# Seven block products in place of eight: the gate and up products of a SwiGLU layer on one Trainium2 core

## The chip, the cores and the metric

The kernel runs on one core of one Trainium2 chip. The metric is the time of one execution on the device, in microseconds. TensorE appears as PE in the rows (its weight loads as PEld), VectorE as DVE, ScalarE as ACT, GpSimd as POOL, and SyncE, which issues nearly all transfers, as SP.

## The reference

One layer over 512 latent tokens of width 2048, with 256 context tokens, all in float32:

```python
h = modulate(rms_norm(x, norm_mix), mod[:, 0], mod[:, 1])
p = h @ w_in                        # then three mixers, merged and projected by w_out
x = x + mod[:, 2] * latent_mixer(p, rope, k_ctx, v_ctx, lw)
h2 = modulate(rms_norm(x, norm_ffn), mod[:, 3], mod[:, 4])
x = x + mod[:, 5] * swiglu(h2, lw)

def swiglu(h, lw):
    return (jax.nn.silu(h @ lw["w_ffn_gate"]) * (h @ lw["w_ffn_up"])) @ lw["w_ffn_down"]
```

The change concerns the last two lines of the layer. `w_ffn_gate` and `w_ffn_up` are 2048 x 5632, `w_ffn_down` is 5632 x 2048.

## The kernel before, in words

Channels lie on the 128 partitions and tokens along the free axis, so the moving operand of a product is 128 channels x 512 tokens and the stationary operand a 128 x 128 block of a weight. Every float32 operand is split into two fp32r parts: ScalarE casts it to `hi`, VectorE subtracts to get `lo` (`split_load`, lines 69 and 70, for weights; `split_to`, lines 82 and 83, for other tiles). A product is then three matmuls into the same PSUM bank, `hi*hi`, `lo*hi` and `hi*lo` (`mm3`, lines 77 to 79).

`proj_pair` (line 523) makes 256 output channels: it loads four 128-row blocks of a weight (512 KB) with one transfer, splits them, and runs 24 matmuls on them. Its staging tiles `raw`, `whi` and `wlo` have three buffers each. Weights come on SP's queue.

After the output projection `w_out` (tile `pwo`, line 829) the kernel sums squares over all channels (`pms`), takes the reciprocal root on GpSimd, spreads it over the partitions with four small matmuls into `ptb` (line 856), and makes the normalised and modulated tokens `h2h`/`h2l` tile by tile: one multiply on VectorE, one biased copy on ScalarE, one fused subtract on VectorE (lines 865 to 867).

The feed-forward part then runs in 11 chunks of 512 hidden channels. `gate_up(c)` makes the gate (`pfg`) and up (`pfu`) products, applies silu, multiplies and splits the result. `down(c - 1)` multiplies the chunk before with `w_ffn_down` and adds it, scaled, to the residual `xn`, which stays in SBUF. In the last chunk each finished pair of channels is transposed back (`pto`) and stored.

The scheduler of the framework orders the instructions of each engine from its own estimate. Only in stretches marked `manual_schedule` does an engine keep the order of the source; the feed-forward part has none before.

Of the kernel before, what the change touches and what calls it, by code (L numbers as in the profile page):

```python
# [18 lines left out]
P = 128  # L19
T = 512  # L20
D = 2048
KT = D // P
# [11 lines left out]
def hybrid_block(ctx: ExitStack, tc: tile.TileContext, I, out):  # L34
# [83 lines left out]
    spg = [dram.tile([P, 512], F32, name=f"spg{i}") for i in range(KT)]  # L118

# [693 lines left out]
    ex.close()  # L813
    ex = ExitStack()
    ep = ex.enter_context(tc.tile_pool(name="ep2", bufs=2, side="right", reuse_waits="tile"))
    xn = [None] * 8
# [3 lines left out]
    pms = bank("tp", "pms", 2)  # L820

# [4 lines left out]
    for j in range(8):  # L826
        xr = ep.tile([P, 2, 512], F32, tag="xr", name="xr", bufs=2)
        nc.sync.dma_start(xr, spx[j])
        po = proj_pair(I["w_out"][0], 256 * j, KT, mk, "pwo")
        xn[j] = yt(f"xn{j}", F32)  # L830
        xa[j] = ep.tile([P, 2, 512], F32, tag="xa", name=f"xa{j}", bufs=8)
        if j == 7:
            sumsq(sqa, True, False)
        for n in range(2):
            kt = 2 * j + n
            nc.vector.scalar_tensor_tensor(xn[j][:, n], po[n], modc[:, 0, kt:kt + 1], xr[:, n], op0=mul, op1=add)
            if kt == 0:
                nc.scalar.activation(sqa, xn[j][:, n], AF.Square)
            else:
                s = t2("sq2")  # L840
                nc.scalar.activation(s, xn[j][:, n], AF.Square)
                if j < 7:
                    nc.gpsimd.tensor_tensor(sqa, sqa, s, op=add)
                else:
                    sumsq(s, False, n == 1)
        for n in range(2):
            nc.scalar.activation(xa[j][:, n], xn[j][:, n], AF.Copy, scale=a2[:, 2 * j + n:2 * j + n + 1])
# [10 lines left out]
    h2h, h2l = [], []  # L858
    for c in range(8):
        h2h.append(act(f"h2h{c}", F32R))  # L860
        h2l.append(act(f"h2l{c}", F32R))
        for j in range(2):
            kt = 2 * c + j
            u = t2("u2")
            nc.vector.tensor_tensor(u, xa[c][:, j], rb2, op=mul)
            nc.scalar.activation(h2h[c][:, j], u, AF.Identity, bias=modc[:, 1, kt:kt + 1])  # L866
            nc.vector.scalar_tensor_tensor(h2l[c][:, j], u, modc[:, 1, kt:kt + 1], h2h[c][:, j].bitcast(F32), op0=add, op1=sub)

    def h2k(kt):
        return h2h[kt // 2][:, kt % 2], h2l[kt // 2][:, kt % 2]  # L870

    ex.close()
    ep = act2x.enter_context(tc.tile_pool(name="ep3", bufs=2, side="right", reuse_waits="tile"))

    def gate_up(c):
        r = []
        for i in range(2):
            n0 = c * 512 + i * 256
            pg = proj_pair(I["w_ffn_gate"][0], n0, KT, h2k, "pfg")
            sg = []  # L880
            for n in range(2):
                s = ep.tile([P, 512], F32, tag="sg", name="sgf", bufs=4)
                nc.scalar.activation(s, pg[n], AF.Silu)
                sg.append(s)
            pu = proj_pair(I["w_ffn_up"][0], n0, KT, h2k, "pfu")
            for n in range(2):
                nc.vector.tensor_tensor(sg[n], sg[n], pu[n], op=mul)
                ah = ep.tile([P, 512], F32R, tag="fah", name="fah", bufs=8)
                al = ep.tile([P, 512], F32R, tag="fal", name="fal", bufs=8)
                split_to(ah, al, sg[n])  # L890
                r.append((ah, al))
        return r

    def down(c, a, last):
        for j in range(8):
            pp = [bank("ps", "pfd", 6) for _ in range(2)]
            ww = wblk(I["w_ffn_down"][0], 4 * c, 4, 256 * j, 256)
            for k in range(4):
                for n in range(2):
# [71 lines left out]
```

## Time and profile before

| what | us |
|---|---|
| median of 3 runs (3002.25 to 3008.63) | 3006.44 |
| time of the profiled execution | 3006.67 |
| its span, first to last instruction | 3004.8 |
| PE busy | 2927.7 (97%) |
| DVE, ACT, POOL busy | 1359.5, 913.3, 221.4 |

The profiled execution took 1.87 us more than its span, and stands 0.2 us above the median. PE's busy time is made of modelled ends, so a busy PE is read from how far apart its matmuls start and not from their durations.

### The profile page before, as it was taken

The page shows a single profiled execution, that of the slowest core. Times are in us where ns is not written, and L with a number is a line of the kernel's source. Part 1 is how long each engine was busy: PE and PEld are TensorE (multiplying, and loading weights), DVE is VectorE, ACT ScalarE, POOL GpSimd, SP SyncE. Part 2 cuts the span into 40 slices and gives each one's busy share as a digit, 9 for nine tenths or more (in the row PEclk, how much of TensorE's full clock was granted, in tenths as well). Part 3 has the DMA queues.
Part 4 walks back from the last instruction along what each step waited for, and adds up shares of the span by engine and source line. Part 5 has one row for each costly group of instructions (what it writes and reads, how often), then busy time and mean ns, then how long its engine had stood idle before and what let it go on. Part 6 is the DMA issues. An engine that isn't in the chain of part 4 may idle for free.

```text
span 3004.8 us, 33589 instructions
## 1 busy us (share of the span) xinstructions
PE 2927.7 (97%) x13426; PEld 2430.5 (81%) x13426; DVE 1359.5 (45%) x1749; ACT 913.3 (30%) x1377; POOL 221.4 (7%) x211
## 2 busy tenths in 40 slices
PE   7899999999999989999999999999999999999999
PEld 5678888877788778878878888888888888888887
DVE  7946554444445467753342243332423333243334
ACT  6634222222222276632332222222222222222221
POOL 4500000000000042221100000000000000000000
PEclk9999999999999999999999999999999999999999
DMA  8853666665566510154323333332333333333333
GB/s 284 274 172 105 195 196 183 198 191 185 182 201 195 164 43 24 50 173 136 121 89 95 95 98 98 98 97 93 98 98 98 98 93 97 98 98 98 94 96 105
DMA packets 320188, 391.27 MB, mean 130 GB/s; under 512 B 14988, under 2 KB 286736, under 8 KB 320032
## 3 DMA queue, kind: packets, MB, share of 16 engines
q1 hardware_dynamic: 319760, 389.02, 41.5%
q8 instruction: 105, 1.72, 0.2%
q14 instruction: 51, 0.42, 0.0%
q10 hardware_dynamic: 208, 0.06, 0.0%
q0 software_dynamic: 64, 0.06, 0.0%
HBM read 372.30 MB, written 16.78 MB: 129 GB/s over the span
## 4 chain that ended last, share of the span: by engine, by line
PE 61%; ACT 1%; DVE 1%; issue 1%; POOL 0%; POOLq 0%; ACTq 0%
PE pfg L77 5%; PE pfg L78 5%; PE pfg L79 5%; PE pfu L78 5%; PE pfu L79 5%; PE pfu L77 5%; PE pfd L77 5%; PE pfd L79 5%; PE pfd L78 5%; PE pwo L77 2%; PE pwo L79 2%; PE pwo L78 2%; PE pym L78 1%; PE pym L79 1%; PE pym L77 1%
## 5 line engine op out<-in xcount | busy, mean ns | idle before, releaser
L69 ACT CAST whi<-raw 128x1024 fp32r<-128x1024 f32 (+3 forms) x480 | 498.6, 1039 | 1655.9 <-PE pfd L79 310.9
L70 DVE TENSOR_TENSOR wlo<-raw,whi 128x1024 fp32r<-128x1024 f32 (+3 forms) x480 | 580.7, 1212 | 841.1 <-ACT whi L69 841.0
L324 DVE SCALAR_TENSOR_TENSOR macc<-raw,silc,macc 128x1024 f32<-128x1024 f32 x120 | 155.2, 1293 | 360.3 <-DMA raw<-in_w_ada_dram 360.2
L78 PE MATMUL pg<-hh,wlo 128*128 128x512 f32 x768 | 300.7, 392 | 11.3 <-DVE wlo L70 11.1
L79 PE MATMUL pg<-hl,whi 128*128 128x512 f32 x768 | 299.8, 390 | 0.0
L77 PE MATMUL pg<-hh,whi 128*128 128x512 f32 x768 | 298.4, 390 | 0.0
L77 PE MATMUL pfg<-h2h,whi 128*128 128x512 f32 x704 | 275.4, 391 | 1.5 <-ACT h2h L866 1.5
L78 PE MATMUL pfg<-h2h,wlo 128*128 128x512 f32 x704 | 275.2, 391 | 0.0
L77 PE MATMUL pfd<-fah,whi 128*128 128x512 f32 x704 | 274.9, 391 | 0.0
L78 PE MATMUL pfd<-fah,wlo 128*128 128x512 f32 x704 | 274.8, 390 | 0.0
L79 PE MATMUL pfd<-fal,whi 128*128 128x512 f32 x704 | 274.4, 390 | 0.0
L78 PE MATMUL pfu<-h2h,wlo 128*128 128x512 f32 x704 | 274.2, 389 | 0.0
L79 PE MATMUL pfu<-h2l,whi 128*128 128x512 f32 x704 | 274.2, 389 | 0.0
L77 PE MATMUL pfu<-h2h,whi 128*128 128x512 f32 x704 | 274.1, 390 | 0.0
L79 PE MATMUL pfg<-h2l,whi 128*128 128x512 f32 x704 | 272.8, 391 | 0.0
L903 DVE SCALAR_TENSOR_TENSOR xn<-pfd,modc,xn 128x512 f32<-128x512 f32 x176 | 126.4, 751 | 207.6 <-PE pfd L79 207.5
L78 PEld LDWEIGHTS pg<-hh,wlo 128*128 128x128 f32 x768 | 144.2, 188 | 46.3 <-DVE wlo L70 16.6
L77 PEld LDWEIGHTS pg<-hh,whi 128*128 128x128 f32 x768 | 144.3, 188 | 29.9
L79 PEld LDWEIGHTS pg<-hl,whi 128*128 128x128 f32 x768 | 144.3, 188 | 29.3
L77 PEld LDWEIGHTS pfg<-h2h,whi 128*128 128x128 f32 x704 | 132.9, 189 | 29.4 <-ACT h2h L866 1.8
L79 PEld LDWEIGHTS pfg<-h2l,whi 128*128 128x128 f32 x704 | 132.8, 189 | 27.6
L78 PEld LDWEIGHTS pfg<-h2h,wlo 128*128 128x128 f32 x704 | 132.8, 189 | 27.4
(334 smaller groups left out, 4502.6 us busy)
## 6 DMA issues: line engine op xcount, KB each, us to landing
raw<-in_w_in_dram SPq DMA_DIRECT2D x128, 512.0 KB, 4.5
raw<-in_w_ada_dram SPq DMA_DIRECT2D x128, 512.0 KB, 4.0
raw<-in_w_ffn_gate_dram SPq DMA_DIRECT2D x88, 512.0 KB, 3.5
raw<-in_w_ffn_up_dram SPq DMA_DIRECT2D x88, 512.0 KB, 3.5
raw<-in_w_ffn_down_dram SPq DMA_DIRECT2D x88, 512.0 KB, 3.5
raws<-in_w_ada_dram SPq DMA_DIRECT2D x128, 256.0 KB, 4.4
raw<-in_w_out_dram SPq DMA_DIRECT2D x32, 512.0 KB, 3.5
raw<-in_w_mla_out_dram SPq DMA_DIRECT2D x16, 512.0 KB, 3.7
```

The lines of the kernel that those rows point to most:

```text
L69: nc.scalar.copy(hi, raw)
L70: nc.vector.tensor_tensor(lo, raw, hi.bitcast(F32), op=sub)
L77: nc.tensor.matmul(ps, a[0], b[0], start=start, stop=False)
L78: nc.tensor.matmul(ps, a[1], b[0], start=False, stop=False)
L79: nc.tensor.matmul(ps, a[0], b[1], start=False, stop=stop)
L324: nc.vector.scalar_tensor_tensor(mod_acc[0], raw, silc[:, kt:kt + 1], mod_acc[0], op0=mul, op1=add)
L903: nc.vector.scalar_tensor_tensor(xn[j][:, n], pp[n], modc[:, 3, kt:kt + 1], xn[j][:, n], op0=mul, op1=add)
```

## The change

The gate and up products are written as block products. The 256 contraction rows and 256 output channels of a weight make 2 x 2 blocks of 128 x 128, and the 256 contraction rows and 512 tokens make 2 x 2 blocks of 128 x 256. Instead of the 8 products of such blocks, 7 products of sums of blocks are made (Winograd's form), each still as three fp32r matmuls, now with 256 columns. The sums of weight blocks (`wsum`, 4 for each 2 x 2) are made on GpSimd in `form_w`; the sums of token blocks (`ta`, `tb`, 4 for each 2 x 2) on GpSimd in `form_t`, once for the whole stage, into eight tiles `mv`. `recombine` puts the seven results (`sp`, four PSUM banks) together with one copy on ScalarE and six additions on VectorE.

A group is the work on one transfer of weights: `products` runs 2 x 7 x 3 = 42 matmuls. Four groups (`c`) make one block of 256 channels of gate or up; 22 pairs of blocks make 176 groups. In each step of the loop over groups the source loads the weights four groups ahead, forms those two groups ahead, does one part of a waiting recombination, makes one more `mv` tile in the first six steps, and then issues the products. From the sum of squares to the end of this loop all engines keep the order of the source. The first gate block and the first up block take turns, group by group.

PSUM no longer has room for the down product beside it, so the activations are written to DRAM (`spf`), the residual too (`spn`), and after the loop a separate stage reads them back (`aload`), splits them, and multiplies with `w_ffn_down` in four runs of 12, 12, 10 and 10 contraction blocks.

```diff
+    MS = (0, 3, 2, 5, 4, 6, 1)
...
+    G = []
+    for j in range(NP):
+        gs = [(w, j, c) for w in (0, 1) for c in range(4)]
+        G += sorted(gs, key=lambda g: g[2]) if j == 0 else gs
...
+            raws[i] = wpool.tile([P, 2, 4, P], F32, tag="raw", name="raw", bufs=2)
...
+    def form_w(i):
+        if i < len(G):
+            r = raws.pop(i)
+            f = wpool.tile([P, 2, 4, P], F32, tag="wsum", name="wsum", bufs=2)
+            nc.gpsimd.tensor_tensor(f[:, :, 0:2], r[:, :, 1:3], r[:, :, 3:4].broadcast_to([P, 2, 2, P]), op=add)
+            nc.gpsimd.tensor_tensor(f[:, :, 2], f[:, :, 0], r[:, :, 2], op=add)
+            nc.gpsimd.tensor_tensor(f[:, :, 3], f[:, :, 2], r[:, :, 0], op=add)
+            hi = wpool.tile([P, 2, 7, P], F32R, tag="fhi", name="whi")
+            lo = wpool.tile([P, 2, 7, P], F32R, tag="flo", name="wlo")
+            split_to(hi[:, :, 0:3], lo[:, :, 0:3], r[:, :, 0:3])
+            split_to(hi[:, :, 3:7], lo[:, :, 3:7], f)
...
+    order.enter_context(tc.manual_schedule())
...
+    def form_t():
...
+        nc.vector.tensor_tensor(h, h, rbs.unsqueeze(1).broadcast_to([P, 2, 512]), op=mul)
         for j in range(2):
...
+            nc.scalar.activation(h[:, j], h[:, j], AF.Identity, bias=modc[:, 1, 2 * c + j:2 * c + j + 1])
...
+        nc.gpsimd.tensor_tensor(ta, b[:, 3:4].broadcast_to([P, 2, 256]), b[:, 1:3], op=sub)
+        nc.gpsimd.tensor_tensor(tb[:, 1], b[:, 1], ta[:, 1], op=sub)
+        nc.gpsimd.tensor_tensor(tb[:, 0], b[:, 0], tb[:, 1], op=sub)
+        m = mpool.tile([P, 2, 7, 256], F32R, tag="mv", name=f"mv{c}")
+        split_to(m[:, 0, 0:3], m[:, 1, 0:3], b[:, 0:3])
+        split_to(m[:, 0, 4:6], m[:, 1, 4:6], ta)
+        split_to(m[:, 0, 3:7:3], m[:, 1, 3:7:3], tb)
...
+    def products(sp, hi, lo, c):
+        for u in range(2):
+            m = mv[2 * c + u]
...
+            for f in range(7):
+                o = sp[:, f]
+                nc.tensor.matmul(o, hi[:, u, f], m[:, 0, MS[f]], start=first and f % 2 == 0, stop=False, skip_group_check=True)
+                nc.tensor.matmul(o, lo[:, u, f], m[:, 0, MS[f]], start=False, stop=False, skip_group_check=True)
+                nc.tensor.matmul(o, hi[:, u, f], m[:, 1, MS[f]], start=False, stop=last, skip_group_check=True)
+
+    def recombine(sp, out):
...
+        nc.scalar.copy(wk[:, 0], sp[:, 2])
+        nc.vector.tensor_tensor(wk[:, 1], sp[:, 5], wk[:, 0], op=sub)
+        nc.vector.tensor_tensor(wk[:, 2:4], sp[:, 3:5], wk[:, 1:2].broadcast_to([P, 2, 256]), op=add)
+        yield
+        nc.vector.tensor_tensor(out[:, 0], sp[:, 0], wk[:, 0], op=add)
+        nc.vector.tensor_tensor(out[:, 1], sp[:, 6], wk[:, 2], op=sub)
+        nc.vector.tensor_tensor(out[:, 2], sp[:, 1], wk[:, 3], op=add)
+        nc.vector.tensor_tensor(out[:, 3], sp[:, 4], wk[:, 2], op=add)
+        yield
...
+            nc.gpsimd.tensor_tensor(g, g, o, op=mul)
+            nc.sync.dma_start(spf[j], g)
...
+    form_t()
+    form_t()
+    sps, closing = {}, []
+    for i, (w, j, c) in enumerate(G):
+        load_w(i + 4)
+        form_w(i + 2)
+        if closing:
+            if next(closing[0], 0) == 0:
+                closing.pop(0)
+        if i < 6:
+            form_t()
+        if c == 0:
+            sps[w, j] = psp.tile([P, 8, 256], F32, tag="sp", name=("pfg", "pfu")[w])
+        products(sps[w, j], *forms.pop(i), c)
+        if c == 3:
+            closing.append(close_block(w, j, sps.pop((w, j))))
...
+    def aload(j):
...
+        nc.sync.dma_start(raw.rearrange("p a (b n) -> p (a b) n", b=2), spf[j])
+        split_to(hi, lo, raw)
...
+    runs = ((0, 6), (6, 6), (12, 5), (17, 5))
+    nxt = [aload(j) for j in range(6)]
```

On VectorE, at the start of the feed-forward part, before (`u` and `h2l` belong to the eight pairs of normalised tokens, one pair for each number of `xa`):

```order
L865 TENSOR_TENSOR u_12308<-xa_11318,ptb 128x512
L865 TENSOR_TENSOR u_12312<-xa_11318,ptb 128x512
L865 TENSOR_TENSOR u_12318<-xa_11452,ptb 128x512
L867 SCALAR_TENSOR_TENSOR h2l_12307<-u_12308,modc,h2h_12306 128x512
L867 SCALAR_TENSOR_TENSOR h2l_12307<-u_12312,modc,h2h_12306 128x512
L865 TENSOR_TENSOR u_12322<-xa_11452,ptb 128x512
```

The same place on VectorE now:

```order
L909 COPY rbs<-ptb 128x512
L926 TENSOR_TENSOR xa_11351<-xa_11351,rbs 128x1024
L83 TENSOR_TENSOR mv_12397<-xa_11351,mv_12397 128x768
L83 TENSOR_TENSOR mv_12397<-ta,mv_12397 128x512
L83 TENSOR_TENSOR mv_12397<-tb,mv_12397 128x2x256
L926 TENSOR_TENSOR xa_11486<-xa_11486,rbs 128x1024
L83 TENSOR_TENSOR mv_12412<-xa_11486,mv_12412 128x768
L83 TENSOR_TENSOR mv_12412<-ta,mv_12412 128x512
L83 TENSOR_TENSOR mv_12412<-tb,mv_12412 128x2x256
L83 TENSOR_TENSOR wlo<-raw,whi 128x2x384
L83 TENSOR_TENSOR wlo<-wsum,whi 128x2x512
L926 TENSOR_TENSOR xa_11623<-xa_11623,rbs 128x1024
```

Before, the multiplies ran ahead of the subtracts that belong to other tiles; now the multiply of a pair stands behind the last subtract of the pair before, and from the third pair on also behind the two subtracts of a weight form.

On GpSimd at the same place there was nothing before after the reciprocal root. Now (`ta`, `tb` are sums of token blocks, `wsum` sums of weight blocks):

```order
L99 TENSOR_TENSOR rs<-ms,mhalf 128x4
L932 TENSOR_TENSOR ta<-xa_11351 128x512
L933 TENSOR_TENSOR tb<-xa_11351,ta 128x256
L934 TENSOR_TENSOR tb<-xa_11351,tb 128x256
L932 TENSOR_TENSOR ta<-xa_11486 128x512
L933 TENSOR_TENSOR tb<-xa_11486,ta 128x256
L934 TENSOR_TENSOR tb<-xa_11486,tb 128x256
L845 TENSOR_TENSOR wsum<-raw 128x2x256
L846 TENSOR_TENSOR wsum<-wsum,raw 128x2x128
L847 TENSOR_TENSOR wsum<-wsum,raw 128x2x128
L932 TENSOR_TENSOR ta<-xa_11623 128x512
```

Two token pairs come first, then one weight form and one token pair in turn, until all eight pairs are made.

On SP's queue, where the loop ends and the down stage begins, the rows now read (`araw` is an activation tile read back, `xd` a residual tile, `spf_170` the last activation tile written):

```order
L838 DMA raw<-in_w_ffn_up_dram 128x4x256
L1014 DMA araw<-spf_149 128x1024
L1014 DMA araw<-spf_150 128x1024
L1014 DMA araw<-spf_151 128x1024
L1027 DMA xd_22543<-spn_141 128x1024
L66 DMA raw<-in_w_ffn_down_dram 128x4x256 x3
L1027 DMA xd_22645<-spn_142 128x1024
L1027 DMA xd_22747<-spn_143 128x1024
L1027 DMA xd_22849<-spn_144 128x1024
L1027 DMA xd_22951<-spn_145 128x1024
L1014 DMA araw<-spf_152 128x1024
L976 DMA spf_170<-fg 128x1024
```

Behind these stand `xd`, `araw`, `xd` and `araw`, in turn; the second of them is the sixth activation tile, which the first two output blocks need, and then come the weights of the second pair. Before, the weights of the down product followed those of gate and up in the same queue, eight transfers for each chunk, and nothing was read back.

## Rows read from the trace of the kernel before

**Rows 1.** Busy time of each engine, share of the span, instructions (the page).

```profile
PE 2927.7 (97%) x13426; PEld 2430.5 (81%) x13426; DVE 1359.5 (45%) x1749; ACT 913.3 (30%) x1377; POOL 221.4 (7%) x211
```

**Rows 2.** Stretch, length, busy PE, PEld, DVE, ACT, POOL, PE clock, DMA share, GB/s.

```profile
1543.50:1552.80 9.30, 5.05 (x33) 4.53 (x31) 4.65 (x11) 4.09 (x7) 1.02 (x1) 0.72 0.19 57
1552.80:1558.00 5.20, 5.19 (x13) 4.14 (x14) 5.20 (x9) 3.24 (x5) 0.00 (x0) 0.51 0.00 0
1558.00:2900.00 1342.00, 1342.00 (x5922) 1112.14 (x5921) 471.75 (x496) 313.82 (x344) 0.00 (x0) 1.00 0.31 97
0.00:150.00 150.00, 121.80 (x492) 89.49 (x492) 121.02 (x166) 93.48 (x116) 74.02 (x37) 0.93 0.86 279
```

**Rows 3.** One of six like groups of gate and up matmuls: line, form, count | busy, mean.

```profile
L77 PE MATMUL pfg<-h2h,whi 128*128 128x512 f32 x704 | 275.4, 391 | 1.5 <-ACT h2h L866 1.5
```

**Rows 4.** 256-column matmuls in a row, first and last of 11: start, us, engine, line.

```profile
1257.65 0.28 PE L77 MATMUL avps<-PT,vh 128*128 128x256 f32 x1
1258.84 0.28 PE L78 MATMUL avps<-PT,vl 128*128 128x256 f32 x1
```

**Rows 5.** 258-column matmuls, first and last of 17.

```profile
273.04 0.29 PE L77 MATMUL gp<-whi,Fh 128*128 128x258 f32 x1
274.96 0.28 PE L78 MATMUL gp<-whi,Fl 128*128 128x258 f32 x1
```

**Rows 6.** Weight loads of that stretch.

```profile
273.04 0.19 PEld L78 LDWEIGHTS gp<-whi,Fl 128*128 128x128 f32 x1
273.17 0.19 PEld L79 LDWEIGHTS gp<-wlo,Fh 128*128 128x128 f32 x1
```

**Rows 7.** Start of the feed-forward part: start, us, engine, instruction [idle before].

```profile
1549.23 2.04 PE L856 MATMUL ptb<-dg,ones 128*128 128x128 f32 x8 [1.76 <-DVE dg L855]
1551.31 1.88 DVE L865 TENSOR_TENSOR u<-xa,ptb 128x512 f32<-128x512 f32 x3 [1.64 <-PE ptb L856]
1552.03 1.34 ACT L866 ACTIVATE h2h<-u,modc 128x512 fp32r<-128x512 f32 x2 [5.06 <-DVE u L865]
1552.81 0.80 PE L77 MATMUL pfg<-h2h,whi 128*128 128x512 f32 x1 [1.54 <-ACT h2h L866]
```

**Rows 8.** GpSimd adds, 512 and 1024 wide: count, min/median/max ns.

```profile
L843 POOL TENSOR_TENSOR sqa<-sqa,sq x13: 1288/1304/1766, 1394.1 to 1525.4; 128x512 f32<-128x512 f32 x13
L261 POOL TENSOR_TENSOR wlo<-raws,whi x24: 2337/2772/4350, 19.0 to 146.7; 128x1024 fp32r<-128x1024 f32 x24
```

**Rows 9.** GpSimd beside VectorE, twice: start, us, instruction.

```profile
75.31 5.73 POOL L261 TENSOR_TENSOR wlo<-raws,whi 128x1024 fp32r<-128x1024 f32 x2 [2.76 <-PE gv L271]
76.80 2.00 DVE L261 TENSOR_TENSOR wlo<-raws,whi 128x1024 fp32r<-128x1024 f32 x1 [0.91 <-ACT whi L259]
...
1303.61 1.37 DVE L806 TENSOR_TENSOR lg<-lg,pym 128x512 f32<-128x512 f32 x2 [2.45 <-PE pym L79]
1305.38 1.37 DVE L70 TENSOR_TENSOR wlo<-raw,whi 128x1024 fp32r<-128x1024 f32 x1 [0.40 <-ACT whi L69]
1304.38 3.52 POOL L807 TENSOR_TENSOR la<-la,lg 128x512 f32<-128x512 f32 x2 [7.34 <-DVE lg L806]
```

**Rows 10.** VectorE and ScalarE operations by form: count | busy, mean ns.

```profile
L70 DVE TENSOR_TENSOR wlo<-raw,whi 128x1024 fp32r<-128x1024 f32 x459 | 563.5, 1230 | 817.3 <-ACT whi L69 817.3
L83 DVE TENSOR_TENSOR fal<-sgf,fah 128x512 fp32r<-128x512 f32 x44 | 28.3, 684 | 0.0
L83 DVE TENSOR_TENSOR atl<-avps,ath 128x256 fp32r<-128x256 f32 x16 | 6.8, 422 | 4.0 <-ACT ath L82 3.9
L214 DVE COPY rbc<-ptb 128x512 f32<-128x512 f32 x1 | 0.7, 683 | 0.0
L69 ACT CAST whi<-raw 128x1024 fp32r<-128x1024 f32 x459 | 483.2, 1053 | 1624.2 <-PE pfd L79 310.9 <-PE pfu L79 288.1 <-PE pfg L79 224.1
L82 ACT CAST fah<-sgf 128x512 fp32r<-128x512 f32 x44 | 25.0, 616 | 0.0
```

**Rows 11.** Transfers of gate weights: count, KB, median us from issue to landing (the page).

```profile
raw<-in_w_ffn_gate_dram SPq DMA_DIRECT2D x88, 512.0 KB, 3.5
```

More of the change, by code (lines that the diff above doesn't have):

```diff
@@ L118, in hybrid_block @@
     spg = [dram.tile([P, 512], F32, name=f"spg{i}") for i in range(KT)]
+    spn = [dram.tile([P, 2, 512], F32, name=f"spn{i}") for i in range(8)]
+    spf = [dram.tile([P, 4, 256], F32, name=f"spf{i}") for i in range(DFF // 256)]
     actx = ExitStack()
@@ L869, in h2k @@
[L869 to L892, printed above, removed]
@@ L894, in down @@
-    def down(c, a, last):
-        for j in range(8):
-            pp = [bank("ps", "pfd", 6) for _ in range(2)]
-            ww = wblk(I["w_ffn_down"][0], 4 * c, 4, 256 * j, 256)
-            for k in range(4):
-                for n in range(2):
-                    mm3(pp[n], (ww[0][:, k, tk(n)], ww[1][:, k, tk(n)]), a[k], k == 0, k == 3)
+    rbs = tmp.tile([P, 512], F32, tag="junk", name="rbs", bufs=1)
+    nc.vector.tensor_copy(rbs, rb2)
+    ex.close()
+    psx.close()
+    act2x.close()
@@ new lines, in products @@
+    def products(sp, hi, lo, c):
+        for u in range(2):
+            m = mv[2 * c + u]
+            first, last = c + u == 0, c == 3 and u == 1
+            for f in range(7):
[3 more added lines that the diff above has]
+                nc.tensor.matmul(o, hi[:, u, f], m[:, 1, MS[f]], start=False, stop=last, skip_group_check=True)
@@ new lines, in hybrid_block, with close_block @@
+    halves = {}
+    def close_block(w, j, sp):
+        o = yt(("fg", "fu")[w], F32).rearrange("p a (b n) -> p (a b) n", b=2)
+        yield from recombine(sp, o)
+        if w == 0:
+            nc.scalar.activation(o, o, AF.Silu)
+            halves[j] = o
+        else:
+            g = halves.pop(j)
+            nc.gpsimd.tensor_tensor(g, g, o, op=mul)
[16 more added lines that the diff above has]
+            closing.append(close_block(w, j, sps.pop((w, j))))
@@ new lines, in hybrid_block @@
+    for x in closing:
+        for _ in x:
+            pass
+    order.close()
+    psx.close()
+    mx_.close()
+    wx.close()
+    dx = ExitStack()
+    apool = dx.enter_context(tc.tile_pool(name="apool2", bufs=24, reuse_waits="tile"))
+    stage = dx.enter_context(tc.tile_pool(name="stage4", bufs=3, reuse_waits="tile"))
+    ep = dx.enter_context(tc.tile_pool(name="ep4", bufs=2, side="right", reuse_waits="tile"))
+    psx = ExitStack()
+    psp = psx.enter_context(tc.tile_pool(name="ps5", bufs=6, space=PS, reuse_waits="tile"))
@@ L917, in down @@
                 nc.sync.dma_start(out[:, 256 * j:256 * j + 256].rearrange("(t p) d -> p t d", p=P), ot)
[L919 to L925 removed]
     psx.close()
[L927 removed]
+    dx.close()
 _INS = ["x", "c", "ctx", "c_ctx", "w_ada", "b_ada", "norm_mix", "norm_ffn", "w_in", "b_gate", "q_a_norm", "kv_a_norm",
```

92 lines of the change are left out of this document (64 added, 28 removed).

## The prediction

> **What bounds the kernel now.** I read the busy time by engine first, then the table by stretches, and last the rows of the stage that changes. PE is busy 97% of the span, DVE 45%, ACT 30%, POOL 7% [rows 1]. In the long stretch of the feed-forward part PE has no idle time at the full clock: 5922 matmuls in 1342.00 us, one every 0.2266 us [rows 2]. That step, and not the modelled 391 ns of a row, is the price of a 512-column matmul. Weights arrive at a DMA share of 0.31, so nothing but PE bounds this stage. What the change takes from PE is therefore gained in full, as long as the others keep up and the new joints are no dearer.
>
> **PE's own work.** Gate and up are six groups of 704 matmuls [rows 3], 4224 x 0.2266 = 957.2 us. The change makes 176 groups of 42, that is 7392 matmuls of 256 columns. Before has these forms: 11 matmuls of 256 columns start 1.19 us apart from first to last, 0.119 each [rows 4], and 17 of 258 columns take 16 steps in 1.92 us, 0.120 each [rows 5]. At 0.119 the new stage is 879.6 us, or 5.0 us a group: 77.6 us less. At 0.120 it would be 70.2 less. A weight load has a row of 0.19 us, longer than such a step, but the loads too start 0.13 and less apart [rows 6], so they overlap and do not set the step.
> What the trace shows of the loads speaks against a rule of the Trainium skill (page "TensorE: Matmul & The Clock Gate", section "Part 3: Packing small matmuls — row/col tiling"), that a weight load overlaps with matmuls in flight only in another row group of the array. By that rule load and matmul would add up; it stands below as a rival.
>
> **The start of the stage.** Before, PE's first gate matmul comes at 1552.81, 1.54 us after the spread of the reciprocal root ended, because one multiply (DVE) and one biased copy (ACT) are enough for it [rows 7]. The clock is then at 0.51 for 5.2 us, in which 12 matmuls run instead of 24 [rows 2]; that costs before about 2.5 us.
> Now each token pair needs a longer chain, and the fixed orders put the next pair's multiply behind the last subtract of this pair, and the sums of a weight form between. Prices:
> - POOL: 1.30 for a 512-wide add, 2.34 for 1024 without disturbance [rows 8]. A 256-wide add is not in the trace. Its bounds are 0.65 (half of 1.30) and 1.30; I take 0.77, on the line through the two rows. One form, of weights or of tokens, is 1.30 + 2 x 0.77 = 2.84.
> - POOL and DVE do not read SBUF together: two 1024-wide POOL subtracts took 5.73 us, 1.05 more than 2 x 2.34, and the DVE subtract that began at 76.80 between them took 2.00 instead of 1.23. At 1304.38 two POOL adds took 3.52, 0.94 more than 2 x 1.29, around another such subtract [rows 9, 10]. So a DVE subtract with both inputs in SBUF holds POOL up by about 1.0 us for 1024 elements, and waits for whole POOL operations itself.
> - DVE 1.23 and ACT 1.05 for 1024 elements, 0.68 and 0.62 for 512 [rows 10], two biased copies 1.34 [rows 7].
> One token pair: multiply 1.23, copies 1.34, POOL 2.84, held up by the first two subtracts (768 + 512 elements) 1.25, cast 0.62, subtract 0.68: 8.0 us. With a weight form between: 1.23 + 1.34 + 2.84 + 1.25, then the form's 2.84 and 1.25 for the subtracts of 512 and 768 elements that stand against it, then cast 1.05 and subtract 1.23 of the sums: 13.0 us. Without any collision it would be 10.5; with the subtracts at their whole durations 13.6.
> A copy of the root from PSUM (0.68) comes first, so the chain begins at 1552.0. The pairs' multiplies start at 0, 8.0 and then every 13.0 us; the eighth starts at 86.0 and its tile is whole 8.6 us later, at 1646.6. PE cannot end group 6 and run group 7 before that. Those 63 matmuls take 9.8 us if the first 5.2 us run at the low clock, as after the gap before: end at 1656.4. In an undisturbed stream from 1552.8 these eight groups would end at 1592.8. **Start: +63.6, less the 2.5 that before pays itself, +61.**
> Then group 8 needs the PSUM of the first gate block. The last four additions that free it stand on DVE behind the form of group 10, and that form needs the buffer which PE frees with the end of group 7 (three buffers): cast, subtract, cast of the sums and their subtract, about 3.1, and 4 additions of 0.42 [rows 10]. **+5** (bounds 3 and 8).
>
> **The other 168 groups.** Per group POOL has 2.84, DVE subtracts of 1792 elements that hold the port 1.75: 4.59. In eight groups there are also one 1024-wide product on POOL, 2.34, in sum 39.1 us against PE's 40.0. ACT and DVE alone need less. So PE still sets the pace, with 2% to spare; two groups of forms in advance absorb one product of 2.34. I allow 0.05 us a group, **+8**. The bounds are 0 and, at 1.30 for each 256-wide add, 47.5 us in eight groups, +158; that end I hold for unlikely, as the two POOL rows differ by 1.04 for 512 elements.
> In the rows the PSUM-reading multiply `lg` beside the POOL add at 1304.38 kept its pace, 1.37 for two [rows 9]. The Trainium skill (page "SBUF — State Buffer", section "Who interferes with whom") says the same in general: a VectorE operation with at most one SBUF input does not contend with GpSimd. That counts here, since the twelve additions of a pair's recombination have one input in PSUM: 5.6 us in eight groups. By the rule they lie beside POOL; if they held the port too, the sum would be 44.7 us and the term +99 instead of +8.
>
> **The turn to the down stage.** The first read-back tile lies where the last `mv` tiles were, so nothing of it can start before PE's last block product. Behind it on SP's queue stand 16 more transfers of 512 KB up to the sixth activation tile, which the first output pair needs. A weight transfer lands 3.5 us after its issue [rows 11], and in the fullest stretch 279 GB/s were moved [rows 2], 1.88 us for 512 KB. So the fifth, the first weights, lands 11.0 after PE's end and PE starts at about 13.3; the seventeenth lands at 33.6. Cast, subtract and the last eight matmuls (1.8) end at 37.7, where 72 matmuls at 0.2266 are 16.3. **+21.** Bounds: 13, if only the first matmul waits, and 30, if transfers under way share the rate evenly.
>
> **What else moves.** Forms 0 and 1 lie in the output projection; there POOL and ACT wait long for PE, and I price them at 0; if they are not hidden, 4 us. The residual's writes and reads are 16 transfers, hidden but for the turn, as is the read-back of later runs: 44 transfers of 1.88 in the first run against 130 us of PE. The 2112 down matmuls, the transposes and the tail stay. DVE has 64 evictions of `pfd` instead of 176; it was not the bound, so nothing is gained.
>
> **Sum.** -77.6 + 61 + 5 + 8 + 21 = +17 on the profiled execution's 3006.7, which is 0.2 above the median of the runs: about 3024.
>
> **Rivals.**
> - POOL alone paces the start (faster than before). If the other engines' parts of a step lie beside POOL's, a step is two forms of 2.84, 5.7 us in place of 13.0: 6 x 7.3 = 44 us less, 2980. It decides from a step below 9, where the sum is 24 us smaller and the time 3000. For it: POOL has the longest rows there, and ACT and DVE are free for half of a step. Against: the rows of the order put the next pair's multiply behind the sums of the weight form, which POOL makes last, and even without collisions that chain is 10.5, 3009. 0.14, a cheaper turn or stream with it counted in.
> - POOL and DVE together bound the stream. If adds or PSUM inputs hold the port longer, 0.3 to 0.6 us are lost in each of 168 groups: 3024 + 42 to 93, 3066 to 3117. For it: the spare is 2%. Against: the rows of the two meetings. 0.15.
> - A weight load and a matmul of 256 columns do not overlap: 0.19 + 0.119 would make 2284 us of the 880, about 4430. The rows of 256 columns at 0.119, each with its own load, speak against it. That is the rule named above; the trace does not bear it out for this pattern. 0.01.
> - The losses just eat the gain: 3001 to 3012. 0.15.
>
> **How the numbers follow.** My forecast has 0.55, with its own range 3012 to 3055. A measurement of this kernel tells 0.2%, 6 us, from no change. Faster takes the first rival, 0.14; same the last, 0.15; slower the rest, 0.71. The range 2994 to 3090 leaves out half of the first rival and part of the second.
>
> **What would show it.** In the profile after: block products 0.119 apart; POOL, ACT and DVE taking turns in the first 100 us of the stage, with PE about half idle; a gap of some 5 us before the ninth group; then PE without idle time; a gap of 13 us before the first down matmul and short waits on read-back tiles in the next 25. It is wrong if PE idles through the stream, if the first eight groups end within 70 us, or if the turn costs under 10.

## The result and the profile after

The changed kernel took 3023.01 us (median of 5 runs, 3015.22 to 3029.15) against 3006.68 before (5 runs): ratio 1.0053, 95% interval 1.0034 to 1.0072. The forecast was 3024. The sum behind it was not as good as its total: its terms came to +17.4, the stage it spoke of costs +6.5, and the rest of the difference lies in front of any instruction that was changed.

The profiled execution took 3029.15 us, the slowest of the five; its span is 3027.4, 22.6 more than before. The page's busy times answer to [rows 1]:

```profile
PE 2890.0 (95%) x16594; PEld 2544.7 (84%) x16594; DVE 1727.0 (57%) x2020; ACT 1075.5 (36%) x1585; POOL 1037.7 (34%) x785
```

PE is busy 38 us less, POOL 816 more. Where the time went is seen when the span is cut at one instruction that both kernels have, the first matmul of the sums of squares that close the output projection. First of the kernel before, then of the changed one, the rows of that tile; the two times are the first and the last start:

```profile
L824 PE MATMUL pms<-ones,sqa x8: 165/250/251, 1543.5 to 1544.1; 128*128 128x1 f32 x8
```

```profile
L866 PE MATMUL pms<-ones,sqa x8: 164/250/250, 1559.5 to 1560.2; 128*128 128x1 f32 x8
```

16.0 us of the 22.6 have been lost by then, 6.5 come behind it (3004.8 - 1543.5 = 1461.3 against 3027.4 - 1559.5 = 1467.9). The 16.0 are already there at the first matmul of the attention's output projection, 1279.80 against 1295.85, ahead of which both kernels have the same instructions in the same order on PE, DVE, ACT and POOL. The waits of PE in the gate stage have grown, `pg` for `wlo` from 11.1 to 18.8 us.

Three stretches of the changed kernel (columns as in [rows 2]): the first eight groups, a piece of the stream (the groups behind them), and a piece of the turn to the down stage:

```profile
1570.00:1673.00 103.00, 61.84 (x336) 54.96 (x336) 61.87 (x55) 42.32 (x57) 66.38 (x54) 0.73 0.15 46
1800.00:2480.00 680.00, 680.00 (x5669) 680.00 (x5669) 522.37 (x475) 272.17 (x321) 605.32 (x423) 1.00 0.38 118
2524.00:2536.00 12.00, 3.83 (x8) 2.63 (x9) 11.83 (x13) 6.83 (x8) 3.22 (x1) 0.58 0.86 307
```

In the stream PE has no idle time; 5669 block products in 680 us are one every 0.120 us, 5.04 us a group. In the first 103 us PE is busy for 62, at a mean clock of 0.73. All that PE waited for from there to the end (engine, line, releaser: us in total, times, longest):

```profile
PE pfg L947 <- ACT mv L82: 32.4, 12, 4.9
PE pfg L949 <- DVE mv L83: 6.7, 13, 0.9
PE pfg L947 <- DVE fg L961: 5.7, 1, 5.7
PE pfd L77 <- ACT whi L69: 4.2, 1, 4.2
PE pfd L78 <- DVE wlo L70: 4.2, 1, 4.2
PE pfu L947 <- DVE fu L961: 0.6, 1, 0.6
PE pto L1047 <- DVE xd L1040: 0.4, 2, 0.2
```

The first two rows are the start, the third is the ninth group, the next two are the turn, the sixth is all that PE waited in the stream, and the last is the end of the kernel. One step of the start, from one pair's multiply to the next (start, us, engine, instruction, idle before):

```profile
1600.42 1.22 DVE L926 TENSOR_TENSOR xa<-xa,rbs 128x1024 f32<-128x1024 f32 x1
1601.68 1.33 ACT L928 ACTIVATE xa<-xa,modc 128x512 f32<-128x512 f32 x2 [2.43 <-DVE xa L926]
1603.09 1.26 POOL L932 TENSOR_TENSOR ta<-xa 128x512 f32<-128x512 f32 x1 [4.92 <-ACT xa L928]
1604.43 1.32 POOL L933 TENSOR_TENSOR tb<-xa,ta 128x256 f32<-128x256 f32 x1
1605.83 1.05 POOL L934 TENSOR_TENSOR tb<-xa,tb 128x256 f32<-128x256 f32 x1
1606.84 1.26 POOL L845 TENSOR_TENSOR wsum<-raw 128x512 f32<-128x512 f32 x1
1608.18 1.06 POOL L846 TENSOR_TENSOR wsum<-wsum,raw 128x256 f32<-128x256 f32 x1
1609.32 1.33 POOL L847 TENSOR_TENSOR wsum<-wsum,raw 128x256 f32<-128x256 f32 x1
1610.68 1.05 ACT L82 CAST whi<-wsum 128x1024 fp32r<-128x1024 f32 x1 [2.42 <-POOL wsum L847]
```

Each of these rows begins where the one above ends: one chain through three engines, with the other casts and subtracts beside it. The next multiply starts at 1612.90, 12.5 us behind this one.

### The profile page after: what moved, and what is told of

It is laid out like the page before. It is cut to its first block, busy times and chain, and to the rows that moved or that the text cites. A ratio compares the mean times of both kernels' runs of the same rounds, so it can differ in the third digit from the quotient of the medians.

```text
span 3027.4 us, 41323 instructions
## 1 busy us (share of the span) xinstructions
PE 2890.0 (95%) x16594; PEld 2544.7 (84%) x16594; DVE 1727.0 (57%) x2020; ACT 1075.5 (36%) x1585; POOL 1037.7 (34%) x785
## 3 DMA queue, kind: packets, MB, share of 16 engines
q8 instruction: 130, 2.13, 0.3%
## 5 line engine op out<-in xcount | busy, mean ns | idle before, releaser
L69 ACT CAST whi<-raw 128x1024 fp32r<-128x1024 f32 (+4 forms) x312 | 314.6, 1009 | 964.2 <-PE pfd L79 312.2
L70 DVE TENSOR_TENSOR wlo<-raw,whi 128x1024 fp32r<-128x1024 f32 (+4 forms) x312 | 366.5, 1179 | 383.4 <-ACT whi L69 383.1
L947 PE MATMUL pfg<-mv,whi 128*128 128x256 f32 x1232 | 357.6, 290 | 38.1 <-ACT mv L82 32.4
L83 DVE TENSOR_TENSOR wlo<-wsum,whi 128x1024 fp32r<-128x1024 f32 x176 | 318.9, 1812 | 93.4 <-ACT whi L82 93.3
L949 PE MATMUL pfg<-mv,whi 128*128 128x256 f32 x1232 | 357.8, 290 | 6.8 <-DVE mv L83 6.7
L948 PE MATMUL pfg<-mv,wlo 128*128 128x256 f32 x1232 | 355.5, 289 | 0.0
L947 PE MATMUL pfu<-mv,whi 128*128 128x256 f32 x1232 | 349.0, 283 | 0.6 <-DVE fu L961 0.6
L948 PE MATMUL pfu<-mv,wlo 128*128 128x256 f32 x1232 | 348.9, 283 | 0.0
L949 PE MATMUL pfu<-mv,whi 128*128 128x256 f32 x1232 | 348.8, 283 | 0.0
L78 PE MATMUL pg<-hh,wlo 128*128 128x512 f32 x768 | 301.4, 392 | 19.0 <-DVE wlo L70 18.8
L845 POOL TENSOR_TENSOR wsum<-raw 128x512 f32<-128x512 f32 x176 | 279.9, 1590 | 73.4 <-DMA raw<-in_w_ffn_gate_dram 36.8
L78 PE MATMUL pfd<-ah,wlo 128*128 128x512 f32 x704 | 275.9, 392 | 4.2 <-DVE wlo L70 4.2
L77 PE MATMUL pfd<-ah,whi 128*128 128x512 f32 x704 | 275.8, 392 | 4.2 <-ACT whi L69 4.2
```

Of the source, the lines that this page charges most:

```text
L69: nc.scalar.copy(hi, raw)
L70: nc.vector.tensor_tensor(lo, raw, hi.bitcast(F32), op=sub)
L77: nc.tensor.matmul(ps, a[0], b[0], start=start, stop=False)
L78: nc.tensor.matmul(ps, a[1], b[0], start=False, stop=False)
L83: nc.vector.tensor_tensor(lo, src, hi.bitcast(F32), op=sub)
L845: nc.gpsimd.tensor_tensor(f[:, :, 0:2], r[:, :, 1:3], r[:, :, 3:4].broadcast_to([P, 2, 2, P]), op=add)
```

## Experiments

The length from the sums of squares to the end of the span is the same to 0.2 us in both profiles of the changed kernel, so local effects are read from it; whole times also hold the part in front. One part of it is the same work in six of the runs with block products, from the last block product to the end, and took 502.7 to 504.0 us there: a difference of 1 us in local length says nothing by itself.

| kernel | instructions | sums of squares start | from there to the end | median of the runs | ratio to before (95%) |
|---|---|---|---|---|---|
| before | 33589 | 1543.5 | 1461.3 | 3006.7 | |
| changed | 41323 | 1559.5 | 1467.9 | 3023.0 | 1.0053 (1.0034 to 1.0072) |
| changed, again | 41323 | 1549.7 | 1467.7 | 3021.2 | 1.0050 (1.0037 to 1.0062) |
| before plus writes | 33640 | 1534.7 | 1461.0 | 3005.5 | 0.9997 (0.9987 to 1.0007) |
| spread ahead | 41331 | 1552.2 | 1448.1 | 3002.2 | 0.9992 (0.9982 to 1.0003) |
| more on POOL | 41489 | 1553.3 | 1623.5 | 3178.6 (one run) | |
| turn, forms ahead | 41327 | 1551.4 | 1464.7 | 3020.4 | 1.0049 (1.0034 to 1.0063) |
| start and turn | 41253 | 1556.2 | 1438.8 | 2993.6 | 0.9960 (0.9946 to 0.9974) |
| recombine first | 41242 | 1554.4 | 1459.1 | 3015.3 (one run) | |
| before, longer | 49058 | 1550.3 | | 4658.6 | |
| fewer blocks | 33423 | 1543.0 | 1063.6 | 2608.4 | |
| turn, recombine early | 41249 | 1553.2 | 1437.5 | 2995.3 | 0.9964 (0.9953 to 0.9974) |
| token sums on DVE | 41236 | 1547.0 | 1439.7 | 2993.6 | 0.9963 (0.9950 to 0.9977) |

**The time in front of the change.** Four runs.

The changed kernel again, without an edit:

> The changed kernel once more, nothing edited. In its first profile the first matmul of the attention's output projection comes 16.0 us later than in the profile before (1295.85 against 1279.80), although no instruction ahead of it was changed, and from there to the end the changed kernel is only 6.5 us longer. Theory A: those 16 us are one draw of a spread that the loads of the gate stage always have; then the second profile has that matmul anywhere from 1280 to 1296, and the median over these runs lies nearer to 3013 than to 3023. Theory B: something in the changed program delays the unchanged part each time (its larger scratch in DRAM, its longer program); then the matmul comes at 1292 to 1298 again and the median stays at 3018 to 3026.

The median stayed at 3021.23 (3019.19 to 3022.93), as B says, but the projection's first matmul came at 1286.2, where A has it and not B. The spread that A speaks of exists, 10 us between the two profiles, and yet the runs do not come down to 3013.

The kernel before with the change's scratch:

```diff
+        nc.sync.dma_start(spn[j], xn[j])
...
+                nc.sync.dma_start(spf[2 * c + i][:, 2 * n:2 * n + 2].rearrange("p a b -> p (a b)"), sg[n])
```

> The kernel before, with the change's scratch tensors in DRAM and its writes alone: the residual pair after each output projection step and the product of gate and up are also written out (30 tensors, 16 MB); nothing reads them back, and the products stay as before. Theory A (spread of the run): first matmul of the attention's output projection at 1276 to 1284, the whole 3002 to 3010, since 16 MB more lie beside a DMA share of 0.3. Theory B, first form (the added scratch moves addresses and slows the loads of the gate stage): that matmul at 1290 or later and the whole 3012 or more. Theory B, second form (the longer program): as A.

The time did not change: 3005.47, with the matmul at 1271.0, earlier than either theory had it. The scratch tensors and 16 MB of writes cost nothing. Left was the length of the program. The kernel before, with matmuls appended that run when all else is done:

```diff
...
+    pe = bank("tp", "pend", 2)
+    for _ in range(3867):
+        nc.tensor.matmul(pe[:, 0:1], xn[7][:, 1, tk(3)], ones[:, :1], start=True, stop=True)
...
```

> The kernel before with 3867 matmuls of one column appended behind its last output pair (their result is not used), so that the program has about as many instructions as the changed one; the work up to there is untouched. It is read by the start of the sums of squares that close the output projection: 1543.5 and 1534.7 us in the two profiles with the products of before, 1559.5, 1549.7, 1552.2 and 1553.3 in the four profiles with block products, though the instructions and their order are the same up to the last steps of the attention's projection. Theory A: a longer program alone delays the gate stage's loads; the sums start at 1547 or later. Theory B: the length has no part in it; they start at 1534 to 1546. The appended matmuls take 150 to 500 us, so the whole time is no measure.

And the other way round, the changed kernel cut short: it makes 12 of the 22 pairs of blocks and leaves the other ten out.

```diff
-    for j in range(NP):
+    NQ = 12
+    for j in range(NQ):
...
-        nc.sync.dma_start(raw.rearrange("p a (b n) -> p (a b) n", b=2), spf[j])
+        nc.sync.dma_start(raw.rearrange("p a (b n) -> p (a b) n", b=2), spf[j % NQ])
```

> The changed kernel with 12 of the 22 gate and up blocks left out of... rather kept: blocks 13 to 22 are not computed, and the down stage reads the first 12 again in their place, so that the program is about as short as the one before. It is read by the start of the sums of squares that close the output projection: 1543.5 and 1534.7 us in the two profiles of the shorter programs with the old products, 1550.3 in the one of the old products with 3867 matmuls appended, 1549.7 to 1559.5 in seven of the block products; and by the spread of the runs about the profiled one, since all behind that point has a constant length. Theory A (the length of the program decides): the sums start at 1546 or earlier. Theory B (something else in the changed program): 1548 or later. The whole is about 2616 us, 80 groups of 5.06 less than 3021, either way.

The same tile's rows of the four kernels, in this order: changed again, before plus writes, before but longer, changed with fewer blocks:

```profile
L866 PE MATMUL pms<-ones,sqa x8: 164/250/250, 1549.7 to 1550.4; 128*128 128x1 f32 x8
```

```profile
L826 PE MATMUL pms<-ones,sqa x8: 164/250/250, 1534.7 to 1535.4; 128*128 128x1 f32 x8
```

```profile
L824 PE MATMUL pms<-ones,sqa x8: 164/250/250, 1550.3 to 1550.9; 128*128 128x1 f32 x8
```

```profile
L867 PE MATMUL pms<-ones,sqa x8: 164/250/250, 1543.0 to 1543.7; 128*128 128x1 f32 x8
```

Both came out as A: the old products in a long program are late, the new ones in a short program are as early as before. The profiles with at most 33640 instructions have 1534.7, 1543.0 and 1543.5, the ten with 41236 and more 1547.0 to 1559.5. If each run's span less the constant part behind is taken as this point (e.g. 3000.3 - 1448.1), the medians over the runs are 1543 for the short programs and 1550 to 1556 for the long ones: 7 to 13 us, and 9 to 10 for the changed kernel. One of four runs of the short changed kernel comes out at 1553 this way, so the bands touch. That the length of the program goes with it is shown from both sides; by what path it delays an unchanged stage is not, and stays open. More loading of instructions in that stage it is not: between 420 and 1290 us the two queues that load them carry 31 or 32 and 19 packets in the kernel before, the changed one, the long one and the short one alike.

**The start.** The next pair's multiply and copies ahead of this pair's sums:

```diff
+    spread_t()
+    spread_t()
     form_t()
+    spread_t()
     form_t()
...
         load_w(i + 4)
+        if i < 6:
+            spread_t()
         form_w(i + 2)
```

(`spread_t` is the multiply and the two copies, cut out of `form_t`.)

> The changed kernel with the multiply and the two biased copies of the next token pair moved ahead of this pair's weight form and token sums in the order of DVE and ACT; POOL's order stays. Theory A: the 12.5 us from one pair to the next are a chain through three engines, POOL works 7.6 of them; with the chain broken POOL sets the step, 7.6 to 8.5, so the stretch from the copy of the root to the end of the eighth group falls from 100.9 us to 65 to 73, and the time by 28 to 36: 2987 to 2995. Rival B: POOL and DVE hinder each other at the port, so that the work of a step only moves closer together down to 10 to 11 us: 9 to 15 us less, 3008 to 3014. Rival C: the stall at the start is made up for later anyway: within 6 us of 3023.

From the copy of the root to the end of the eighth group it took 83.5 us instead of 100.9, the time fell to 3002.20, 19 less than the changed kernel on the same chip. So the start is what costs, and C falls. The time lies between what A and B had; the step is 10.0 and not 8, as B has it. Rows of one step:

```profile
1596.44 1.74 DVE L926 TENSOR_TENSOR xa<-xa,rbs 128x1024 f32<-128x1024 f32 x1
1597.18 1.60 POOL L940 TENSOR_TENSOR tb<-xa,tb 128x256 f32<-128x256 f32 x1
...
1598.22 1.34 ACT L928 ACTIVATE xa<-xa,modc 128x512 f32<-128x512 f32 x2 [5.13 <-DVE xa L926]
...
1599.46 0.82 ACT L82 CAST whi<-raw 128x768 fp32r<-128x768 f32 x1
...
1600.11 0.74 POOL L846 TENSOR_TENSOR wsum<-wsum,raw 128x256 f32<-128x256 f32 x1
...
1600.31 1.35 DVE L83 TENSOR_TENSOR wlo<-raw,whi 128x768 fp32r<-128x768 f32 x1 [2.13 <-ACT whi L82]
```

Beside each other a multiply takes 1.74 where it took 1.22 in the chain above, and a 256-wide sum 1.60, while one that begins when no DVE operation is under way takes 0.74. The last row is the only place in the step where DVE waits; below it turns out to matter.

The ninth group's wait, with the recombination's parts moved ahead of the weight form in each group's order:

```diff
         load_w(i + 4)
-        form_w(i + 2)
         if closing:
             if next(closing[0], 0) == 0:
                 closing.pop(0)
+        form_w(i + 2)
```

> The changed kernel with the recombination's parts ahead of the weight form in each group's order, nothing else. It is read by the wait before the ninth group alone, 5.71 and 5.80 us in two profiles. Theory A (the prediction's): the four additions that free the first gate block's PSUM stand on DVE behind the subtracts of the eleventh group's form, which waits for PE's eighth group; ahead of it they are done before that group ends, and the wait is 0 to 1 us. Rival B: it is PE's own block that is awaited, or the eleventh form is then late instead: 4 to 6 us in this place or in the two groups behind.

The first product of the ninth group, in the changed kernel and in this one:

```profile
1673.23 0.55 PE L947 MATMUL pfg<-mv,whi 128*128 128x256 f32 x1 [5.71 <-DVE fg L961]
```

```profile
1663.88 0.36 PE L947 MATMUL pfg<-mv,whi 128*128 128x256 f32 x1 [1.45 <-DVE fg L961]
```

1.45 is left, a little over what A allowed. The local length fell by 8.7, twice what the wait fell by. Most of the rest is the clock behind it. The 27 us and the 36 us from about these rows on:

```profile
1673.00:1700.00 27.00, 26.19 (x194) 26.04 (x195) 13.90 (x15) 9.75 (x11) 14.57 (x12) 0.88 0.20 59
```

```profile
1664.00:1700.00 36.00, 36.00 (x301) 36.00 (x302) 27.40 (x26) 16.29 (x19) 30.32 (x22) 1.00 0.39 117
```

At a granted clock of 0.88 there are 194 products in 27 us, where 225 would have fitted, 3.7 us. PE sat idle for 0.8 of that (27.00 less 26.19), 0.6 of it the wait of `pfu` in the list of PE's waits; the other 2.9 are the clock. Behind the short wait the clock is 1.00, and the wait of `pfu` is gone. Wait 4.3, clock 2.9 and `pfu` 0.6 make the 7.8 by which the way from the copy of the root to the last block product got shorter; the remaining 0.9 lies behind it, in work that is the same, and is no more than the spread there. This kernel ran once.

**POOL's room in the stream.** One more addition in each weight form:

```diff
+            if i > 9:
+                jk = t2("jk").rearrange("p (u b n) -> p u b n", u=2, b=2)
+                nc.gpsimd.tensor_tensor(jk, r[:, :, 1:3], r[:, :, 3:4].broadcast_to([P, 2, 2, P]), op=add)
```

> The changed kernel with one more POOL addition of 512 elements in each weight form from the eleventh on (its result is not used). It asks how much room POOL has in the stream, where it is busy 0.89 of the time and PE does not wait. Theory A: most of its rows hold no waiting, a group has 4.5 us of it, so 1.3 to 1.6 more make 5.8 to 6.1 us against PE's 5.06: 166 groups by 0.7 to 1.0, 120 to 175 us longer, 3140 to 3200. Rival B: a third of POOL's busy time is waiting for the port while DVE subtracts, its real need is about 3.6, and one addition more still fits: 0 to 20 us longer.

It took 155.7 us longer behind the sums of squares, 0.94 for each of 166 groups, as A has it. The stream of this kernel:

```profile
1800.00:2480.00 680.00, 609.06 (x4715) 588.03 (x4714) 376.41 (x392) 220.53 (x267) 662.34 (x465) 0.97 0.31 98
```

POOL is busy 97%, PE waits, and a group takes 6.06. An addition that takes 1.27 undisturbed has cost 0.94 to 1.02; at that price POOL had 0.25 to 0.33 us of spare time in 5.04. The prediction had 0.11. That the recombination stands beside POOL without harm is seen in the changed kernel:

```profile
2507.12 1.22 DVE L83 TENSOR_TENSOR wlo<-wsum,whi 128x1024 fp32r<-128x1024 f32 x1 [1.72 <-ACT whi L82]
2507.34 1.61 POOL L846 TENSOR_TENSOR wsum<-wsum,raw 128x256 f32<-128x256 f32 x1
2508.71 0.69 DVE L956 TENSOR_TENSOR wk<-pfg,wk 128x512 f32<-128x512 f32 x1
2509.02 0.74 POOL L847 TENSOR_TENSOR wsum<-wsum,raw 128x256 f32<-128x256 f32 x1
```

Beside a subtract with two inputs in SBUF the sum took 1.61, beside an addition with one input in PSUM 0.74. The Trainium skill (page "SBUF — State Buffer", section "Who interferes with whom") says that a VectorE operation with at most one SBUF input, outside its two-port modes, does not contend with GpSimd. These rows agree, and so do the 35 sums of this width between 1700 and 2500 us that had only such additions beside them: 0.73 to 0.75.

**The turn.** In the changed kernel the first read-back tiles are issued long before PE's last block product, which starts at some 2523.4 (SP's queue):

```profile
2511.13 1.29 SPq L1014 DMA_DIRECT2D araw<-spf  x3
2512.47 0.43 SPq L1027 DMA_DIRECT2D xd<-spn  x1
2512.94 2.11 SPq L66 DMA_DIRECT2D raw<-in_w_ffn_down_dram  x3
```

What PE waited for then is work, not a transfer:

```profile
2523.73 0.37 ACT L954 COPY wk<-pfu 128x256 f32<-128x256 f32 x1 [9.21 <-PE pfu L949]
2524.00 2.94 ACT L82 CAST ah<-araw 128x1024 fp32r<-128x1024 f32 x3
2526.53 5.66 DVE L83 TENSOR_TENSOR al<-araw,ah 128x1024 fp32r<-128x1024 f32 x3
2526.76 3.22 POOL L975 TENSOR_TENSOR fg<-fg,fu 128x1024 f32<-128x1024 f32 x1 [17.00 <-DVE fu L961]
2526.84 2.94 ACT L69 CAST whi<-raw 128x1024 fp32r<-128x1024 f32 x3
2527.94 1.22 PE L77 MATMUL pfd<-ah,whi 128*128 128x512 f32 x2 [4.24 <-ACT whi L69]
2533.39 0.79 PE L78 MATMUL pfd<-ah,wlo 128*128 128x512 f32 x1 [4.23 <-DVE wlo L70]
```

The read-back tiles land 3.4 to 8.0 us from their issue, before 2521, but their casts stand behind the last block's copy in ACT's order. Three of each put ahead of it (the three lines on `closing` stood before the down stage's tiles):

```diff
-    for x in closing:
-        for _ in x:
-            pass
...
+    nxt, pre = [], {}
+    for j in range(3):
+        nxt.append(aload(j))
+        pre[j] = wblk(wd, 4 * j, 4, 0, 256)
+    for x in closing:
+        for _ in x:
+            pass
...
```

> The changed kernel with the first three read-back tiles and the first three weights of the down stage loaded, cast and subtracted ahead of the last block's recombination in the order of ACT and DVE. Theory A: at the turn no transfer is late (the first read-back is issued 12.6 us before PE's last block product, not behind it as the prediction had it); PE's two waits of 4.24 and 4.23 us are the queues of ACT and DVE, where the weight's cast stands behind the last block's copy and three casts, and its subtract behind four additions and three subtracts, and the low clock after them costs about 3.3 more. Then both waits fall under 1 us and the time by 9 to 12: 3009 to 3013. Rival B: the read-back or its tiles do wait for PE's last products, so the casts can't move; the waits stay at 3 to 5 us each and the time within 4 us of 3021.

Neither was right, though the time, 3020.40, is within B's 4 us. The second wait went, the first became 6.43, and 3.1 us of local length were gained where A had 9 to 12 of time:

```profile
2519.33 1.21 DVE L83 TENSOR_TENSOR al<-araw,ah 128x1024 fp32r<-128x1024 f32 x1
2522.05 0.41 DVE L961 TENSOR_TENSOR fu<-pfu,wk 128x256 f32<-128x256 f32 x1
2522.61 0.77 PE L77 MATMUL pfd<-ah,whi 128*128 128x512 f32 x1 [6.43 <-DVE fu L961]
```

The down product also needs the PSUM of the last up block, and the additions that free it now stood behind the moved subtracts on DVE. Two tiles and two weights ahead, the recombination next (the edit is to the version with all edits, which follows below):

```diff
     for j in range(3):
+        if j == 2:
+            for x in closing:
+                for _ in x:
+                    pass
         nxt.append(aload(j))
         pre[j] = wblk(wd, 4 * j, 4, 0, 256)
-    for x in closing:
-        for _ in x:
-            pass
```

> The version with the four edits, and at the turn only two read-back tiles and two weights are cast and subtracted ahead of the last recombination, the third of each behind it. In the run with all three ahead PE's first down product waited 6.43 us for the last addition that frees the PSUM of the last up block, because that addition stood behind the subtracts on DVE. Theory A: the PSUM sets the turn; the recombination alone takes 2.9 us (copy 0.37, subtract 0.42, addition 0.69, four additions of 0.42, less their overlap), so the wait is 2.7 to 3.2 and the time 3 to 4 less than that version's: 2990. Rival B: the third tile and weight, now behind, make PE wait again: a second wait of 2 to 5 us, and no gain.

The wait became 3.16, as A has it, and a second of 2.21 for a read-back tile's cast appeared, as B has it. The local length is 1.3 us less than that of the version below, 0.4 of it behind the last block product, and the medians are 2995.3 and 2993.6: no gain is shown.

**All of it together.** The three edits above with three tiles ahead at the turn, and the sums of the third pair on written into a finished pair's memory:

```diff
-        ta = t2("ta").rearrange("p (a n) -> p a n", a=2)
-        tb = t2("tb").rearrange("p (a n) -> p a n", a=2)
+        ta = (t2("ta") if c < 2 else xa[c - 2][:, 0]).rearrange("p (a n) -> p a n", a=2)
+        tb = (t2("tb") if c < 2 else xa[c - 2][:, 1]).rearrange("p (a n) -> p a n", a=2)
```

> The changed kernel with four things together: the next pair's multiply and copies ahead (as in the run that had this alone), the token sums of the third pair on in the memory of a pair that is done, so that POOL doesn't wait for the subtract that frees a sum's buffer, the recombination's parts ahead of the weight form, and the turn's casts and subtracts ahead of the last recombination. In the run with the first alone a pair took 9.97 us, in which POOL and DVE were each busy 8.3 and POOL waited 1.56 for such a buffer. Theory A: the step falls to 8.3, 10 us less; the wait before the ninth group goes, 5 less; the turn gives 10: 3002 - 25 = 2977 (2970 to 2984). Rival B: POOL and DVE, once they are never apart, hold each other up at the port, and the step stays at 9.5 to 10: 2985 to 2990. Rival C: what is taken out here turns up as low clock or as waits in the stream behind it: 2990 to 3000.

2993.63, 0.9960 of before (0.9946 to 0.9974): the first version that beats both kernels, but 17 us short of A. The buffer was not the limit: the pairs of this kernel start 9.5 to 11.2 us apart, the last three steps 10.2 on average. Of the 9.3 us less local length than with the spread alone, the ninth group's wait gave 4.5, the 168 groups behind it 2.2 (0.6 of a wait, the rest clock) and the turn 3.3; the start took 0.7 more. Last, the token sums on DVE:

```diff
-        nc.gpsimd.tensor_tensor(ta, b[:, 3:4].broadcast_to([P, 2, 256]), b[:, 1:3], op=sub)
+        nc.vector.tensor_tensor(ta, b[:, 3:4].broadcast_to([P, 2, 256]), b[:, 1:3], op=sub)
...
```

> As the run with the early recombination at the turn, and the token sums of the start on DVE instead of POOL. In the version with the four edits a pair takes 10.0 to 11.2 us, with DVE and POOL each busy some 8.3 of them. Theory A: a DVE operation with both inputs in SBUF and a POOL operation hardly run at one time, so that what counts is the sum of their undisturbed rows, POOL 2 x 1.27 + 4 x 0.74 = 5.5 and DVE 5.7: 11.2. Then the move makes POOL 2.75 and DVE 7.2, sum 10.0, and the step becomes 9 to 10, 5 to 8 us less in all. Rival B: each engine only has its own row to go through, with the durations seen: POOL's part falls to about 3.8, DVE's 7.2 sets the step: 7.2 to 8, 14 to 20 us less in all. Rival C: the longer chain on DVE takes it back: 10 or more.

The step is 10.6: C. From the copy of the root to the end of the eighth group it took 83.6 us, as with the sums on POOL; the local length is 2.2 longer, 1.0 of it ahead of that copy. Three different orders have a step of 10.0 to 10.6, with POOL's share going from 8.2 us to 4.4, so neither POOL alone nor the sum of both sets it.

What does stands in DVE's rows. In each step from the fourth pair on, in all three orders, DVE has one gap, 2.12 or 2.13 us, and no other: its first subtract of a weight form waits for ACT's cast of that weight, which stands in ACT's order behind the next pair's two biased copies, and these wait for the multiply on DVE (the rows from 1596.44 to 1600.31 above). For the rest of the step DVE is busy: 7.8 to 7.9 us in the first of the orders, 7.3 to 9.1 in the version with all edits, 7.9 to 8.5 with the token sums. Busy time and gap add up to the step each time. So what was left after the long chain was undone is DVE's own queue, its operations lengthened by POOL's, and one wait for ACT. No run has taken that wait out, so what it is worth is not shown.

## Why the prediction came out right, term by term

- **Products: -77.6 forecast, -70.2 measured.** The step is 0.120, not 0.119: the row with 17 matmuls [rows 5] was the better one of the two. The text named 0.120 and its -70.2 as the other end. A weight load of 0.19 us with each product did overlap, so the rival of 4430 falls.
- **Start and ninth group: +61 and +5 forecast, +62 measured.** The second multiply came 8.1 us behind the first (8.0 forecast), the next ones 12.5 (13.0), the eighth 83.1 (86.0), the ninth group's wait was 5.71 (5). From the copy of the root to the ninth group it is 106.7 us, where eight groups of 5.04 are 40.3; less the 4.0 that before lost there (1.54 and 2.5), 62.4. The 256-wide sum taken as 0.77 is 0.74 undisturbed, and 1.05 to 1.33 in these rows: the collisions were priced as an addition of 1.25 a form and came to 1.0. That the chain and not POOL paces the start was shown by undoing it. Two slips in the text change nothing: [rows 2] has 13 matmuls at the low clock, where 23 would have fitted, and not 12 of 24; and the step with whole subtracts adds up to some 13.8, not 13.6.
- **Stream: +8 forecast, +4 measured**, and not for the reason given. PE waits 0.6 us in 168 groups; the rest is the low clock behind the ninth group's wait, about 3 (the 168 groups take 850.3 us there and 846.8 behind the short wait), which the sum had left out.
- **Turn: +21 forecast, some +12 measured.** Here a step failed: "The first read-back tile lies where the last `mv` tiles were, so nothing of it can start before PE's last block product." The first three tiles were issued 12.3 us before it, when PE was halfway through the third group from the end, past the third pair's products, and no transfer that PE waited for was late. What was late is the queue on ACT and DVE and the PSUM of the last block: 4.24 and 4.23, and 3.3 for the low clock behind them. The bound of 13 was nearer, for another reason.
- **What was in no term: +9 to +10, in unchanged code.** The four terms as measured come to +8, and the stage measures +6.5 (0.8 of the difference lies between the sums of squares and the first operation on the spread root, 7.1 us against 7.9 before). The sum was thus 11 too dear, and the total came out by luck: the front part of the longer program is late by about as much. By its own terms the change is worth about 3013, at the upper edge of the rival "the losses just eat the gain". Its 6.5 us are 0.2%, which is just what the prediction took for the least that a measurement can tell; the rest of the 0.5% that was measured lies ahead of the stage that it spoke of.

## What to carry to other kernels

When block products trade matmuls for sums, look first at the few microseconds in which the first operands are made: an order by tile strings three engines into one chain, and moving the next tile's first two operations ahead gave back 17 us here. Then look which queue is left: here DVE's, with one wait for ACT in each step. A stall can cost more than its own length: 4.3 us of wait less gave 7.8, since the granted clock behind the long wait was 0.88 over 27 us and behind the short one 1.00. Cut the span at an instruction that both kernels share before explaining a difference.

## What was not expected of the hardware

Programs of 41236 to 49058 instructions reached the same, unchanged point 7 to 13 us later in the median than programs of 33423 to 33640, whether the extra instructions came behind that point as block products or as matmuls whose result nobody uses. The waits of PE for the gate stage's weights grew with it, 2.4 to 11.1 us in the three short programs and 13.1 to 18.8 in the long ones. And a 256-wide GpSimd sum took 0.74 us in the changed kernel's stream when nothing or only additions with a PSUM input ran beside it, and 1.33 to 1.61 when a VectorE operation with two SBUF inputs was under way as it began; in the start of the stage the latter took 1.05 to 1.33.
